# State-space mixer: the pooling branch by token, its moving means as products with a constant band matrix, and the projected blocks read back on GpSimd's queue

## Chip, cores, metric

One core of a Trainium2 chip runs the whole program. The metric is the device time of one execution in microseconds (us). Engines are named as in the profile: PE is TensorE's matmul stream, PEld its weight loads, DVE is VectorE, ACT is ScalarE, POOL is GpSimd, SP is SyncE, which here only issues DMAs.

## What is computed

The program is a trunk of two layers over 512 tokens of width 1024. Each layer has a SwiGLU network, a mixer and a second SwiGLU network. The change lies in the mixer of layer 0:

```python
z = hn @ ab_w_in[i]                                   # (512, 1024)
ya = pool_mixer(z[..., :512], pool_w[i], pool_scale[i])
yb = s5_mixer(z[..., 512:], ...)                      # bidirectional complex-diagonal scan
m = concatenate([ya, yb], -1) @ ab_w_out[i]

def pool_mixer(u, w_grp, scale):                      # 4 groups of 128 channels
    for gi, w in enumerate((2, 4, 8, 16)):            # windows, centred, cut off at the ends
        start, end = clip(t - w//2, 0, L), clip(t - w//2 + w, 0, L)
        p[gi] = (cs[end] - cs[start]) / (end - start) - u[group gi]
    return einsum('blgc,gcd->blgd', p, w_grp) * scale
```

So the pooling branch takes, for each channel, the mean over a window of tokens minus the token itself, and then a 128x128 product per group.

## The kernel before

Every product of two float32 matrices is written as three products of split operands: hi.hi, lo.hi and hi.lo (`mm3`, L179). ACT makes each hi by a cast, and DVE the lo by subtracting hi from the source. Weights go through the same split in the class `Weights`: `hi` (L117) on ACT, `lo` (L128) on DVE, four or five tiles ahead of their use. Each engine works its own queue strictly in the order in which the Python code issues.

`mixer` (L1335) stands at 393 to 540 us of the span. First, `first_proj` (L362) projects the four state-space blocks; the columns of `xT` (the normed tokens, channels on partitions) are kept in the order "mix", by place in a chunk of 8 tokens and then by chunk. `chunk_rows` (L1365) copies each block out of PSUM on ACT and writes it to `z_dram`; `u_rows` (L1374) reads two blocks at a time back on SP's queue into `us`, eight tokens of a chunk on partitions.

Then four units `ct` of the scan run through five steps: `inject` (L1384, PE: 32 small products from `us` and the table `cm` into the only `ps_x` buffer), `decay` (L1396, ACT), `scan` (L1403, DVE, a generator that yields in three places), `permute` (L1431, ACT) and `output` (L1438, PE 48 small products, then GELU on ACT and a DMA out). In this text a scan has a part A (L1410 and L1411, which read `ps_x`), a part B (L1413, L1414 and four scans L1419) and a part C (L1421, L1422 and four L1427, which write `s`). `inject` of the next unit must wait for part A, since `ps_x` has one buffer.

Between them stands the pooling branch. `pool_tile(i)` (L1468) projects a group on PE (24 products of 512 columns, channels on partitions), copies it twice on ACT with a reordering to plain token order (L1479, L1480), and sums the window by doubling on POOL (L1485, L1489, L1494, L1496); `rest` splits the result on ACT and DVE (L1500, L1501). `pool_out(i)` (L1505) multiplies by the group's 128x128 weights and splits again (L399, L400). `out_a` (L1513) accumulates the output projection. The hand-written order of all this is L1521 to L1581.

Of the kernel before, what the change touches and what calls it, by code (L numbers as in the profile page):

```python
# [7 lines left out]
F32 = mybir.dt.float32  # L8
# [7 lines left out]
P = 128  # L16
# [157 lines left out]
class Builder:  # L174
# [126 lines left out]
    def to_xT(self, xn, pair, gain, order, between, by_tile=False):  # L301
# [12 lines left out]
        for b in range(KT // 2):  # L314
            if not by_tile:
                ps[b] = self.bank("ps_t")
            for kt in (2 * b, 2 * b + 1):
                for i in range(by_tile, 2):
                    transpose(kt, i)
            if b % 2 == 1:  # L320
                for kt in (2 * b - 2, 2 * b, 2 * b - 1, 2 * b + 1):
                    src = ps[kt // 2][:, kt % 2 * 256:(kt % 2 + 1) * 256]
                    if order == "mix":
                        src = src.rearrange("p (c j) -> p j c", j=8)
                    elif order == "att":
                        src = src.rearrange("p (r c) -> p c r", r=4)
                    hi, lo = (self.part(x[:, kt, :], order, pair) for x in self.xT)
                    g = self.gcol[:, gain * KT + kt:gain * KT + kt + 1]
                    nc.scalar.activation(out=hi, in_=src, func=AF.Copy, scale=g)
                    V.scalar_tensor_tensor(out=lo, in0=src, scalar=g, in1=hi.bitcast(F32),  # L330
                                           op0=ALU.mult, op1=ALU.subtract)
            if b == 1 and between:
                between()


    def part(self, x, order, pair):

# [997 lines left out]
    def mixer(self, nxt, before):  # L1335
# [3 lines left out]
        xh, xl = self.xT  # L1339
        edge, scol, bcol = self.mix_small  # L1340
        con = {}
# [14 lines left out]
        def start():  # L1356
            nonlocal yp, y, yhl, sp, us
            yp = tc.alloc_tile_pool(name="mix_y", bufs=1)
            y = yp.tile([P, 4, SEQ], F32, name="y")
            yhl = [yp.tile([P, 4, SEQ], F32R, name=n) for n in ("y_hi", "y_lo")]  # L1360
            sp = tc.alloc_tile_pool(name="mix", bufs=1)
            us = sp.tile([P, 32, 64], F32, name="us")
            load("m0", "e0")

        def chunk_rows(ct, ps):  # L1365

            zt = sp.tile([P, SEQ], F32, tag="yt", bufs=2, name="zt")
            nc.scalar.copy(zt, ps)
            rows = self.z_dram[ct * P:(ct + 1) * P]
            nc.scalar.dma_start(rows, zt)  # L1370
            if ct == 2:
                u_rows(0)

        def u_rows(ct):  # L1374
            nc.sync.dma_start(us[:, 8 * ct:8 * ct + 16], self.by_chunk(self.z_dram[ct * P:(ct + 2) * P]))

        yp = y = yhl = sp = us = None
        self.first_proj(4, "mix", before, start, chunk_rows)
        load("m1")
        u_rows(2)  # L1380
        load("m2", "e1", "i0")
# [85 lines left out]

        def pool_tile(i):  # L1468

            w = self.W.take()  # L1470
            ps = self.bank("ps_p")
            self.proj(ps, w, "mix")
            pad, win = 16, self.POOL_W[i]
            z, s = (sp.tile([P, SEQ + 2 * pad], F32, tag="pz%d" % k, bufs=1, name="pz") for k in range(2))
            p = sp.tile([P, SEQ], F32, tag="pp", bufs=2, name="pp")
            by_token = ps.rearrange("p (j c) -> p j c", j=8)
            G.memset(z[:, :pad], 0.0)
            G.memset(z[:, pad + SEQ:], 0.0)
            nc.scalar.copy(z[:, pad:pad + SEQ].rearrange("p (c j) -> p j c", j=8), by_token)  # L1479
            nc.scalar.activation(out=p.rearrange("p (c j) -> p j c", j=8), in_=by_token, func=AF.Copy,  # L1480
                                 scale=float(win))
            o, e = 0, SEQ + 2 * pad
            for step in range(i + 1):
                if step == 0:
                    G.tensor_tensor(out=s[:, 1:], in0=z[:, 1:], in1=z[:, :-1], op=ALU.add)  # L1485
                    o = 1
                else:
                    h = 1 << (step - 1)
                    G.tensor_tensor(out=s[:, o + h:e - h], in0=z[:, o:e - 2 * h], in1=z[:, o + 2 * h:e], op=ALU.add)  # L1489
                    o, e = o + h, e - h  # L1490
                z, s = s, z
            for k, (a, b) in enumerate(((0, win // 2), (SEQ - win // 2 + 1, SEQ))):
                if b > a:
                    G.tensor_tensor(out=z[:, pad + a:pad + b], in0=z[:, pad + a:pad + b],  # L1494
                                    in1=edge[:, i, 8 * k:8 * k + b - a], op=ALU.mult)
            G.tensor_tensor(out=p, in0=z[:, pad:pad + SEQ], in1=p, op=ALU.subtract)  # L1496

            def rest():
                hl = [v[:, i] for v in yhl]
                nc.scalar.copy(hl[0], p)  # L1500
                V.tensor_tensor(out=hl[1], in0=p, in1=hl[0].bitcast(F32), op=ALU.subtract)  # L1501

            return rest

        def pool_out(i):  # L1505
            ps = self.bank("ps_A" if i < 3 else "ps_p")
            self.mm3(ps, [z[:, i * P:(i + 1) * P] for z in w_pool], [v[:, i] for v in yhl], True, True)
            self.split_evac(xh[:, i], xl[:, i], ps, scol[:, i:i + 1])

# [11 lines left out]
        for i, win in enumerate(self.POOL_W):  # L1521
            G.tensor_scalar(out=scol[:, i:i + 1], in0=scol[:, i:i + 1], scalar1=1.0 / win, scalar2=None, op0=ALU.mult)
        rest = [pool_tile(0)]
        decay(0)
        decay(1)
        inject(0)
        load("g0")
        for _ in scan(0):
            pass
        rest.append(pool_tile(1))  # L1530
        rest[0]()
        decay(2)
        inject(1)
        load("m3", "e2")
        for _ in scan(1):
            pass
        rest.append(pool_tile(2))
        rest[1]()
        permute(0)
        decay(3)  # L1540
        inject(2)
        load("i1", "g1")
        self.W.done()
        output(0)
        turn = scan(2)
        next(turn)
        rest[2]()
        self.W.done()
        y_rows(0)
        load("e3", "g2")  # L1550
        for _ in turn:
            pass
        rest.append(pool_tile(3))
        permute(1)
# [10 lines left out]
        rest[3]()  # L1565
        self.W.done()
        permute(2)
        out_a(range(3), range(2))
        next(turn)
        pool_out(3)  # L1570
        for _ in turn:
            pass
        output(2)
        permute(3)
# [3 lines left out]
        y_rows(2)  # L1578
        self.W.done(2)
        output(3)  # L1580
# [61 lines left out]
    def mid_weights(self, ly):  # L1642
        w = self.ins
        if ly == 0:
            l = [w["w_in"][i] for i in (4, 5, 6, 7, 0, 1, 2, 3)] + [w["w_pool"]]
            l += [w["w_ao"][0, i] for i in range(2)] + [w["w_glu"][i] for i in range(2)]
            return l + [w["w_ao"][0, i] for i in (2, 3)] + [w["w_ao"][1, i] for i in range(4)]
# [6 lines left out]
    def build(self):  # L1654
        tc, nc = self.tc, self.nc
        with ExitStack() as ctx:
# [9 lines left out]
            self.mix_small = [self.base.tile([P, *n], F32, name="mix_" + k)  # L1666
                              for k, *n in (("edge", 4, 16), ("scol", 4), ("bcol", 4))]
            self.h = self.base.tile([P, TT, D], F32, name="h")
# [12 lines left out]
    def first_norm(self, gain, order):  # L1681
# [5 lines left out]
        step(1)  # L1687
        edge, scol, bcol = self.mix_small
        nc.gpsimd.dma_start(edge, self.ins["pool_edge"].partition_broadcast(P))
        nc.gpsimd.dma_start(scol, self.ins["pool_sc"])  # L1690
# [61 lines left out]
def lay_out(inputs):  # L1752
# [25 lines left out]

    edge = np.zeros((4, 16), np.float32)
    for i, w in enumerate(Builder.POOL_W):  # L1780
        edge[i, :w // 2] = [w / (t + w // 2) for t in range(w // 2)]
        edge[i, 8:7 + w // 2] = [w / (w - 1 - k) for k in range(w // 2 - 1)]
    lanes = lambda z: z.reshape(2, 16, 2, 64, -1).transpose(2, 3, 0, 1, 4).reshape(P, 32, -1)
# [13 lines left out]
        "glu_b": a["ssm_b_glu"][0].reshape(4, P).T,  # L1797
        "pool_edge": edge,
        "w_in": col_tiles(a["ab_w_in"][0]),
        "w_pool": np.concatenate([a["pool_w"][0].transpose(1, 0, 2).reshape(P, HALF),  # L1800
# [31 lines left out]
```

## Time and profile before

| | us |
|---|---|
| median of 3 runs | 1886.88 (1886.74 to 1887.07) |
| the profiled execution's own time | 1886.41 |
| its span | 1884.6 |
| PE busy | 1831.5 (97%) |
| DVE busy | 1470.7 (78%) |
| ACT busy | 925.7 (49%) |
| POOL busy | 350.4 (19%) |

The span runs from the first to the last instruction; the execution's own time has 1.8 us more around it. Busy shares are means over the whole program: a stage of 70 us can be bound by another engine than the program is.

### The profile page before, as it was taken

Reading aid. Unit: us, or ns where it says so; the run is one execution under the profiler, and the core shown is the slowest. Engines: PE = TensorE matmul, PEld = TensorE weight load, DVE = VectorE, ACT = ScalarE, POOL = GpSimd, SP = SyncE. Lnnn points to the kernel's source line nnn. Section 1 sums busy time; section 2 is a strip of 40 time slices with the busy share of each in tenths; the row PEclk is TensorE's granted clock in tenths of the full one; section 3 lists DMA queues with packets and bytes.
Section 4 is the critical chain, followed back from the end, with each engine's and each line's share of the span. In section 5 each row is a group of like instructions: output and inputs, shape, how many; then the busy total and the mean of one; then the engine's idle time right before and its main releaser. Section 6 shows DMA issues by size and latency. Waiting matters only on the chain.

```text
span 1884.6 us, 31563 instructions
## 1 busy us (share of the span) xinstructions
PE 1831.5 (97%) x12368; PEld 1639.3 (87%) x12368; DVE 1470.7 (78%) x2380; ACT 925.7 (49%) x1749; POOL 350.4 (19%) x238
## 2 busy tenths in 40 slices
PE   7999999998899999999999999999999999999998
PEld 7887987787689999988999998888878789999886
DVE  6888989868779999844899996465565589999744
ACT  5254446354455444543644445355555465444532
POOL 2021322015011233200122320012222012322100
PEclk9999999999999999999999999999999999999999
DMA  6474346647432333332233324323222132333321
GB/s 196 128 224 165 110 137 194 202 132 256 161 125 79 101 112 102 107 107 78 94 109 102 103 89 135 101 80 122 90 93 99 62 106 96 102 106 102 123 96 62
DMA packets 82021, 225.48 MB, mean 120 GB/s; under 512 B 15792, under 2 KB 20048, under 8 KB 80848
## 3 DMA queue, kind: packets, MB, share of 16 engines
q1 hardware_dynamic: 70176, 197.80, 31.8%
q0 software_dynamic: 6960, 23.57, 4.1%
q10 hardware_dynamic: 4736, 2.10, 0.4%
q8 instruction: 97, 1.59, 0.4%
q14 instruction: 52, 0.43, 0.1%
HBM read 206.69 MB, written 18.84 MB: 120 GB/s over the span
## 4 chain that ended last, share of the span: by engine, by line
PE 62%; DVE 7%; ACT 3%; issue 1%; DMA 1%; DVEq 0%; ACTq 0%
PE ps_gu L183 10%; PE ps_gu L182 10%; PE ps_gu L181 10%; PE ps_A L183 3%; PE ps_A L182 3%; PE ps_A L181 3%; PE ps_B L182 3%; PE ps_B L181 3%; PE ps_B L183 3%; PE ps_f L181 3%; PE ps_f L182 2%; PE ps_f L183 2%; DVE w_lo L135 1%; PE ps_qk L899 1%; ACT junk L237 1%
## 5 line engine op out<-in xcount | busy, mean ns | idle before, releaser
L135 DVE TENSOR_TENSOR w_lo<-w_raw,w_hi 128x1024 fp32r<-128x1024 f32 x214 | 283.3, 1329 | 215.8 <-ACT w_hi L124 215.6
L124 ACT CAST w_hi<-w_raw 128x1024 fp32r<-128x1024 f32 (+1 forms) x313 | 262.9, 864 | 286.4 <-PE ps_A L183 71.3
L183 PE MATMUL ps_gu<-xT_hi,w_lo 128*128 128x256 f32 (+1 forms) x1008 | 307.5, 305 | 2.5 <-DVE w_lo L135 2.5
L183 PE MATMUL ps_gu<-xsum,w_lo 128*128 128x256 f32 x1088 | 308.2, 283 | 0.6 <-DVE w_lo L135 0.6
L182 PE MATMUL ps_gu<-xsum,w_hi 128*128 128x256 f32 x1088 | 307.8, 283 | 0.2 <-DVE xsum L518 0.2
L181 PE MATMUL ps_gu<-xsum,w_hi 128*128 128x256 f32 x1088 | 307.6, 283 | 0.0
L181 PE MATMUL ps_gu<-xT_hi,w_hi 128*128 128x256 f32 (+1 forms) x1008 | 304.9, 302 | 0.0
L182 PE MATMUL ps_gu<-xT_lo,w_hi 128*128 128x256 f32 (+1 forms) x1008 | 304.5, 302 | 0.0
L183 PEld LDWEIGHTS ps_gu<-xsum,w_lo 128*128 128x128 f32 x1088 | 208.6, 192 | 0.9 <-DVE w_lo L135 0.8
L182 PEld LDWEIGHTS ps_gu<-xsum,w_hi 128*128 128x128 f32 x1088 | 208.5, 192 | 0.4 <-DVE xsum L518 0.4
L181 PEld LDWEIGHTS ps_gu<-xsum,w_hi 128*128 128x128 f32 x1088 | 208.4, 192 | 0.0
L183 PEld LDWEIGHTS ps_gu<-xT_hi,w_lo 128*128 128x128 f32 x1008 | 190.4, 189 | 15.0 <-DVE w_lo L135 4.1
L181 PEld LDWEIGHTS ps_gu<-xT_hi,w_hi 128*128 128x128 f32 x1008 | 190.2, 189 | 8.5 <-issue 0.9
L182 PEld LDWEIGHTS ps_gu<-xT_lo,w_hi 128*128 128x128 f32 x1008 | 190.2, 189 | 7.3
L135 POOL TENSOR_TENSOR w_lo<-w_raw,w_hi 128x1024 fp32r<-128x1024 f32 x31 | 74.1, 2390 | 562.2 <-ACT w_hi L124 532.1
L109 POOL TENSOR_TENSOR w_u<-w_raw,w_s 128x512 f32<-128x512 f32 x64 | 112.2, 1754 | 354.9 <-ACT w_hi L124 196.3
L124 ACT CAST w_hi<-w_s 128x512 fp32r<-128x512 f32 x136 | 77.8, 622 | 197.3 <-DVE w_s L105 193.5
L105 DVE TENSOR_TENSOR w_s<-w_raw,w_u 128x1024 f32<-128x1024 f32 x68 | 145.8, 2144 | 2.3
L640 POOL TENSOR_TENSOR g<-g,m 128x1024 f32<-128x1024 f32 x34 | 94.6, 2782 | 244.9 <-DVE m L638 244.9
L181 PE MATMUL ps_B<-w_hi,gT 128*128 128x512 f32 x352 | 137.1, 389 | 1.6 <-DVE free L1264 1.6
L183 PE MATMUL ps_A<-w_hi,gT 128*128 128x512 f32 x352 | 137.1, 389 | 1.1 <-DVE gT L693 1.1
L181 PE MATMUL ps_A<-w_hi,gT 128*128 128x512 f32 x352 | 137.3, 390 | 0.0
(376 smaller groups left out, 4251.2 us busy)
## 6 DMA issues: line engine op xcount, KB each, us to landing
w_raw<-in_w_gu_dram SPq DMA_DIRECT2D x106, 512.0 KB, 3.4
w_raw<-in_w_dn_dram SPq DMA_DIRECT2D x88, 512.0 KB, 3.3
w_u<-in_w_gu_dram SPq DMA_DIRECT2D x70, 512.0 KB, 3.7
w_raw<-in_w_qk_dram SPq DMA_DIRECT2D x16, 512.0 KB, 3.3
bias<-in_att_bias_dram SPq DMA_DIRECT2D x16, 512.0 KB, 4.1
w_raw<-in_w_in_dram SPq DMA_DIRECT2D x8, 512.0 KB, 3.3
cm<-m_dram SPq DMA_DIRECT2D x4, 1024.0 KB, 8.7
w_raw<-in_w_ao_dram SPq DMA_DIRECT2D x8, 512.0 KB, 3.9
```

What stands on the lines that cost most here:

```text
L105: tt(out=blocks(s), in0=g[:, :HALF].unsqueeze(1).broadcast_to([P, 2, HALF]), in1=blocks(u)[:, :2], op=ALU.subtract)
L109: (h_engine or self.nc.gpsimd).tensor_tensor(out=z["h"], in0=g[:, HALF:], in1=z["s"][:, HALF:], op=ALU.add)
L124: self.nc.scalar.copy(hi[:, k:k + step], src[:, k:k + step])
L135: (engine or self.lo_engine).tensor_tensor(out=lo[:, :n], in0=src, in1=hi[:, :n].bitcast(F32), op=ALU.subtract)
L181: mm(ps, a[0], b[0], start=start, stop=False)
L182: mm(ps, a[0], b[1], start=False, stop=False)
L183: mm(ps, a[1], b[0], start=False, stop=stop)
L237: self.nc.scalar.activation(out=junk[:, :src.shape[-1]], in_=src, func=AF.Square, scale=scale, accum_out=out)
L640: nc.gpsimd.tensor_tensor(out=rows(f), in0=rows(f), in1=m, op=ALU.mult)
L899: nc.tensor.matmul(ps[:, :n], tq[rows], lo[rows], start=False, stop=True)
```

## The change

The pooling half of `z` is projected with tokens on partitions: `pool_rows` takes `xT` as the stationary operand and the weights (`w_pin`, laid out by rows) as the moving one, 24 products for each of four blocks of 128 tokens, as many as before. `split_evac` splits each block into hi and lo out of PSUM (ACT and DVE). `pool_means(i)` then forms the moving means as products of those blocks with a constant band matrix that comes from DRAM: for each token block two products (hi, lo) of 120 or 128 columns, six of 8 columns for the two ends of the sequence, and two of 8 columns for each neighbour block. That makes 20 products for the first group and 26 for each other one, 98 in all. The POOL work of `pool_tile` and its two ACT copies are gone.

Columns of `xT` are now in plain token order; the reordering moves into the copy of `chunk_rows`. Each projected block is read back by itself on POOL's queue instead of two at a time on SP's. `band` is loaded on POOL's queue in `start` and cast on ACT ahead of the first `chunk_rows`. On SP's queue the load of the second `cm` stands earlier. The lo parts of the pooling branch are collected in `lows` and issued at chosen places of the scans.

```diff
         def start():
...
-            load("m0", "e0")
+            raw = sp.tile([P, 640], F32, name="band")
+            G.dma_start(raw, ins["pool_band"])
+            band = [sp.tile([P, n], F32R, name="band" + k) for k, n in (("_hi", 640), ("_lo", 64))]
+            nc.scalar.copy(band[0], raw)
+            V.tensor_tensor(out=band[1], in0=raw[:, 576:], in1=band[0][:, 576:].bitcast(F32), op=ALU.subtract)
+            load("m0", "e0", "m1")
 
         def chunk_rows(ct, ps):
             zt = sp.tile([P, SEQ], F32, tag="yt", bufs=2, name="zt")
-            nc.scalar.copy(zt, ps)
+            nc.scalar.copy(zt.rearrange("p (j c) -> p j c", j=8), ps.rearrange("p (c j) -> p j c", j=8))
             rows = self.z_dram[ct * P:(ct + 1) * P]
             nc.scalar.dma_start(rows, zt)
-            if ct == 2:
-                u_rows(0)
+            G.dma_start(us[:, 8 * ct:8 * ct + 8], self.by_chunk(rows))
...
+        def pool_rows(ts, kts):
+            for kt in kts:
+                if kt // 2 == len(wz):
+                    wz.append(self.W.take())
+                for t in ts:
+                    if kt == 0:
+                        psz[t] = self.bank("ps_A" if t < 3 else "ps_p")
+                    self.mm3(psz[t], [x[:, kt, t * P:(t + 1) * P] for x in (xh, xl)], [x[:, kt % 2 * HALF:(kt % 2 + 1) * HALF] for x in wz[kt // 2]],
+                             kt == 0, kt == KT - 1)
+
+        def pool_means(i, later):
...
+            for k, (o, n, x, m) in enumerate(l):
+                nc.tensor.matmul(ps[:, o:o + n], x, m, start=k == 0, stop=k == len(l) - 1)
+            self.split_evac(*means[i], ps, None, later)
...
         decay(0)
+        pool_rows((0, 1), range(3))
+        inject(0)
+        pool_rows((0, 1), range(3, KT))
+        for t in range(2):
+            self.split_evac(*zs[t], psz[t], None, lows)
         decay(1)
-        inject(0)
         load("g0")
         for _ in scan(0):
             pass
-        rest.append(pool_tile(1))
-        rest[0]()
-        decay(2)
+        run_lows()
         inject(1)
         load("m3", "e2")
-        for _ in scan(1):
+        pool_rows((2, 3), range(KT))
+        self.W.done(4, fill=False)
+        turn = scan(1)
+        next(turn)
+        permute(0)
+        decay(2)
+        output(0)
+        for t in range(2, TT):
+            self.split_evac(*zs[t], psz[t], None, lows)
+        next(turn)
+        run_lows()
+        y_rows(0)
+        inject(2)
+        for _ in turn:
             pass
...
+        load("i1", "g1")
+        for i in range(4):
+            pool_means(i, lows)
+        self.W.fill(1)
+        load("e3", "g2")
         decay(3)
...
         turn = scan(2)
         next(turn)
...
+        run_lows()
         permute(1)
         inject(3)
         output(1)
...
-        for i in range(3):
-            pool_out(i)
+        for i in range(4):
+            pool_out(i, lows)
+        next(turn)
+        run_lows()
+        for _ in turn:
+            pass
+        self.W.fill(3)
+        self.W.done(fill=False)
         turn = scan(3)
```

On DVE, the second scan (unit 1) and what follows it up to the third. `t` holds the scan's work, `s` its result; `y_lo`, `xT_lo` are lo parts of the pooling branch, `w_lo` that of a weight tile. Before:

```order
L1410 TENSOR_TENSOR t_4430<-ps_x,ce 128x1024
L1411 TENSOR_TENSOR t_4431<-ps_x,ce 128x1024
L1413 TENSOR_TENSOR t_4430<-t_4430,t_4431 128x512
L1414 TENSOR_TENSOR t_4430<-t_4430,t_4431 128x512
L1419 SCALAR_TENSOR_TENSOR t_4430<-rho,t_4430 128x256 x4
L1421 TENSOR_TENSOR t_4431<-t_4430,ce 128x1024
L1422 TENSOR_TENSOR t_4430<-t_4430,ce 128x1024
L1427 TENSOR_TENSOR s<-t_4430,t_4431 64x8x64 x4
L1501 TENSOR_TENSOR y_lo<-pp,y_hi 128x512
L135 TENSOR_TENSOR w_lo<-w_raw,w_hi 128x1024
L1410 TENSOR_TENSOR t_4591<-ps_x,ce 128x1024
```

And with the change:

```order
L1414 SCALAR_TENSOR_TENSOR t_4461<-rho,t_4461 128x256 x4
L393 TENSOR_TENSOR xT_lo<-ps_A,xT_hi 128x512
L393 TENSOR_TENSOR xT_lo<-ps_p,xT_hi 128x512
L1416 TENSOR_TENSOR t_4462<-t_4461,ce 128x1024
L1417 TENSOR_TENSOR t_4461<-t_4461,ce 128x1024
L1422 TENSOR_TENSOR s<-t_4461,t_4462 64x8x64 x4
L135 TENSOR_TENSOR w_lo<-w_raw,w_hi 128x1024
L1405 TENSOR_TENSOR t_4702<-ps_x,ce 128x1024
L1406 TENSOR_TENSOR t_4703<-ps_x,ce 128x1024
L393 TENSOR_TENSOR y_lo<-ps_A,y_hi 128x512 x2
L393 TENSOR_TENSOR xT_lo<-ps_A,xT_hi 128x512
L393 TENSOR_TENSOR xT_lo<-ps_p,xT_hi 128x512
```

Line numbers here are those of the changed kernel: L1405 and L1406 are part A, L1408 to L1414 part B, L1416 to L1422 part C, L393 the lo of `split_evac`. Two lo parts, which read PSUM (token blocks 2 and 3), now stand inside scan 1 between its parts B and C, and those of the means stand inside scan 2 behind its part A.

On ACT, what stands around the first GELU (`yt`) and the first weight cast behind it, in the change:

```order
L1451 ACTIVATE yt<-ps_y 128x512
L1452 DMA y_dram<-yt 128x8x64
L392 CAST xT_hi<-ps_A 128x512
L392 CAST xT_hi<-ps_p 128x512
L392 CAST y_hi<-ps_A 128x512 x2
L392 CAST xT_hi<-ps_A 128x512
L392 CAST xT_hi<-ps_p 128x512
L124 CAST w_hi<-w_raw 128x1024
```

The casts of blocks 2 and 3 stand behind the GELU, and the cast of the weight tile, whose `w_lo` DVE does ahead of scan 2, stands behind the casts of all four means.

## Rows read from the trace of the kernel before

**Rows 1.** Windows of 10 us: PE, PEld, DVE, ACT, POOL busy, PE's clock, DMA; sum of 430:500.
```profile
470.00:480.00 10.00, 4.20 (x37) 3.19 (x33) 9.75 (x13) 5.47 (x8) 0.86 (x1) 0.77 0.74 250
...
sum 70.00, PE 57.04 PEld 48.02 DVE 65.36 ACT 34.83 POOL 23.60; mean PE 8.15 PEld 6.86 DVE 9.34 ACT 4.98 POOL 3.37
```
**Rows 2.** The chain that ended last, 478 to 497 us: start, duration, what.
```profile
482.34 0.60 DVE y_lo L1501
482.94 1.14 DVE w_lo L135
...
487.63 0.64 DVE xT_lo L400
...
493.63 0.45 PE ps_y L1453 x8
```
**Rows 3.** Timeline of DVE: start, duration, what, how many.
```profile
431.69 1.23 DVE L1410 TENSOR_TENSOR t<-ps_x,ce 128x1024 f32<-128x1024 f32 x1 [3.79 <-PE ps_x L1392]
...
434.08 0.69 DVE L1413 TENSOR_TENSOR t<-t,t 128x512 f32<-128x512 f32 x1
...
437.76 1.23 DVE L1421 TENSOR_TENSOR t<-t,ce 128x1024 f32<-128x1024 f32 x1
...
441.20 4.58 DVE L1427 TENSOR_TENSOR s<-t,t 64x512 f32<-64x512 f32 x4
...
488.19 1.21 DVE L1421 TENSOR_TENSOR t<-t,ce 128x1024 f32<-128x1024 f32 x1
...
490.77 2.81 DVE L1427 TENSOR_TENSOR s<-t,t 64x512 f32<-64x512 f32 x4
493.60 1.29 DVE L1466 TENSOR_TENSOR y_lo<-y,y_hi 128x512 fp32r<-128x512 f32 x2
```
**Rows 4.** Timeline of PE, mixer: start, duration, what; idle before in brackets.
```profile
424.10 0.40 PE L182 MATMUL ps_p<-xT_lo,w_hi 128*128 128x512 f32 x1
424.33 0.40 PE L183 MATMUL ps_p<-xT_hi,w_lo 128*128 128x512 f32 x1
...
429.56 2.08 PE L1392 MATMUL ps_x<-us,cm 128*64 128x64 f32 x64
...
478.82 0.80 PE L181 MATMUL ps_A<-w_hi,xT_hi 128*128 128x512 f32 x1 [5.80 <-DVE xT_lo L400]
...
485.45 0.34 PE L1449 MATMUL ps_y<-us,perm 128*64 128x64 f32 x4
...
488.40 0.50 PE L181 MATMUL ps_A<-w_hi,xT_hi 128*128 128x512 f32 x1
...
496.11 0.50 PE L181 MATMUL ps_x<-y_hi,w_hi 128*128 128x512 f32 x1
```
**Rows 5.** Timeline of ACT: a reordering copy, a weight cast, a GELU.
```profile
429.67 1.10 ACT L1479 COPY pz<-ps_p 128x512 f32<-128x512 f32 x1 [3.02 <-PE ps_p L183]
...
455.85 1.03 ACT L124 CAST w_hi<-w_raw 128x1024 fp32r<-128x1024 f32 x1
...
458.19 0.60 ACT L1456 ACTIVATE yt<-ps_y 128x512 f32<-128x512 f32 x1
```
**Rows 6.** Timeline of PE: narrow products; 128*64 means 64 stationary columns.
```profile
409.54 1.96 PE L308 MATMUL ps_t<-ident,xn 128*128 128x128 f32 x16 [0.79 <-ACT xn L297]
411.26 0.36 PE L181 MATMUL ps_p<-xT_hi,w_hi 128*128 128x256 f32 x1
...
1328.69 0.22 PE L181 MATMUL ps_o<-pt_hi,v_hi 128*64 128x128 f32 x1
1328.75 0.22 PE L182 MATMUL ps_o<-pt_lo,v_hi 128*64 128x128 f32 x1
```
**Rows 7.** DMA issues: what, queue, count, KB each, median us to landing.
```profile
z_dram<-zt ACTq DMA_DIRECT2D x4, 256.0 KB, 4.4
...
ssm_tab<-in_ssm_c_dram POOLq DMA_DIRECT2D x1, 512.0 KB, 3.7
...
free<-kept_lp POOLq DMA_DIRECT2D x1, 288.0 KB, 8.7
```

More of the change, by code (lines that the diff above doesn't have):

```diff
@@ L1466, in split_y @@
             V.tensor_tensor(out=lo, in0=y[:, ct], in1=hi.bitcast(F32), op=ALU.subtract)
[L1468 to L1503, printed above, removed]
@@ L1505, in pool_out @@
-        def pool_out(i):
-            ps = self.bank("ps_A" if i < 3 else "ps_p")
-            self.mm3(ps, [z[:, i * P:(i + 1) * P] for z in w_pool], [v[:, i] for v in yhl], True, True)
-            self.split_evac(xh[:, i], xl[:, i], ps, scol[:, i:i + 1])
+        zs = [[x[:, t] for x in yhl] if t < 2 else [x[:, 2 + t] for x in (xh, xl)] for t in range(TT)]
+        means = [[x[:, 2 + i] for x in yhl] if i < 2 else [x[:, 4 + i] for x in (xh, xl)] for i in range(4)]
+        psz, wz = {}, []
+        def pool_rows(ts, kts):
[7 more added lines that the diff above has]
+                             kt == 0, kt == KT - 1)
@@ L1510, in mixer, with pool_out @@
+        def pool_out(i, later):
+            ps = self.bank("ps_A" if i < 3 else "ps_p")
+            self.mm3(ps, [z[:, i * P:(i + 1) * P] for z in w_pool], means[i], True, True)
+            self.split_evac(xh[:, i], xl[:, i], ps, scol[:, i:i + 1], later)
         lhs = lambda kt: (xh[:, kt], xl[:, kt])
@@ L1560, in mixer @@
         w_pool = self.W.take()
-        for i in range(3):
-            pool_out(i)
+        for i in range(4):
[6 more added lines that the diff above has]
+        self.W.done(fill=False)
         turn = scan(3)
         next(turn)
-        rest[3]()
-        self.W.done()
         permute(2)
         out_a(range(3), range(2))
-        next(turn)
-        pool_out(3)
+        output(2)
         for _ in turn:
             pass
-        output(2)
         permute(3)
@@ L1578, in mixer @@
         y_rows(2)
-        self.W.done(2)
+        self.W.fill(4)
         output(3)
@@ L1777, in lay_out, with sums @@
     bias = bias.reshape(16, 4, P, 256).transpose(0, 2, 1, 3)
-    edge = np.zeros((4, 16), np.float32)
+    token = np.arange(P)[:, None]
+    band, ends = np.zeros((P, 4, 144), np.float32), np.zeros((P, 4, 2, 8), np.float32)
     for i, w in enumerate(Builder.POOL_W):
-        edge[i, :w // 2] = [w / (t + w // 2) for t in range(w // 2)]
-        edge[i, 8:7 + w // 2] = [w / (w - 1 - k) for k in range(w // 2 - 1)]
+        def sums(t, o):
+            near = (t >= o - w // 2) & (t < o + w // 2)
+            n = np.minimum(o + w // 2, SEQ) - np.maximum(o - w // 2, 0)
+            return near * (np.float32(w) / n.astype(np.float32)) - np.float32(w) * (t == o)
+        band[:, i] = sums(P + token, P + np.arange(-8, 136)[None])
+        ends[:, i, 0] = sums(token, np.arange(8)[None])
+        ends[:, i, 1] = sums(SEQ - P + token, np.arange(SEQ - 8, SEQ)[None])
     lanes = lambda z: z.reshape(2, 16, 2, 64, -1).transpose(2, 3, 0, 1, 4).reshape(P, 32, -1)
```

66 lines of the change are left out of this document (32 added, 34 removed).

## Prediction, written before the changed kernel had run

> **What bounds the kernel now.** I read the windows of the mixer first. From 430 to 500 us DVE is busy for 65.4 of 70 us and PE for 57.0, and in the slice from 470 to 480 PE is busy for 4.2 of 10 us at a granted clock of 0.77, while DVE has 9.75 [rows 1]. So this stage hangs on DVE, though over the whole program PE is the busiest. The chain of waits says the same: in its last part before the output projection it stands on DVE, and it reaches PE only at 493.6 with the last `output` [rows 2]. The timeline of DVE then gives the prices. The first scan starts at 431.69, the last one ends at 493.60: 61.9 us [rows 3]. One scan left alone takes 2.39 us (part A, 431.69 to 434.08), 3.68 (part B, to 437.76) and 5.41 (part C, 488.19 to 493.60), together 11.5 [rows 3]. Four make 45.9. Four lo parts from the pooling tiles at 0.60, three weight lo parts at 1.14 and four lo parts behind `pool_out` at 0.64 [rows 2] add 8.4. That is 54.3 us of 61.9. The missing 7.6 us are instructions that ran longer beside POOL: the four L1427 took 4.58 us in scan 0, 2.81 us in scan 3, where POOL had nothing to do [rows 3]; POOL was busy for 23.6 us of the stage [rows 1].
>
> **What is removed.** POOL's sums go, and with them these 7.6 us of DVE. The two ACT copies of each pooling tile go too; ACT is busy for 35 of 70 us here [rows 1], so this is worth nothing by itself.
>
> **What is added on DVE.** Four lo parts become eight (four token blocks, four means). At 0.60 that is +2.4 us. DVE's own work becomes 54.3 + 2.4 = 56.7 us, 5.2 less than before.
>
> **What is added on PE.** The projection keeps 96 products of 512 columns at 0.233 us (424.10 to 424.33) [rows 4]. New are the 98 narrow products of the means, each with 128 stationary columns. No row of before shows such a product, so I bound it. With 64 stationary and 128 moving columns the pitch is 0.060 us (1328.69 to 1328.75); 16 transposes with 128 stationary columns took 1.72 us, from 409.54 until the next product began at 411.26, 0.107 each [rows 6]. Between 5.9 and 10.5 us in all. I take 0.107, since the stationary columns are as many, and since the weight load cannot hide behind 8 moving columns.
>
> **Where PE and DVE meet.** The new order makes DVE wait for PE through ACT in places where it waited for nothing. I lay the prices along the queues.
>
> *Start.* The band is loaded on POOL's queue once the transposes, the last readers of the memory under it, have ended: 409.54 + 1.96 = 411.5 [rows 6]. Loads on that queue took 3.7 to 8.7 us [rows 7]; I take 5, which with the issue gives 417. Its cast (estimate 0.7, by the weight cast of 1.03 for 1024 columns [rows 5]) stands ahead of the first block's copy on ACT. That copy now reorders: 1.10 us [rows 5]. Then 4.4 us to `z_dram` [rows 7] and again 5 for the readback: `us` is there at 429.0. PE has done 18 of its products by 428.3 and injects from 429.0 to 431.2 (2.08 [rows 4] and a gap). Before, scan 0 began at 431.7, now at 431.3: -0.4. With the two loads at 3.7 each PE's 428.3 decides (-0.7 more); at 8.7 each it is 435.7, +6.7. In `z_dram`'s wait only the other readbacks queue on POOL, so nothing else there is late.
>
> *First wait.* PE: 30 products (7.0), inject 1 (2.2), 48 products for blocks 2 and 3 (11.2), `output` 0 (2.9, as 485.45 to 488.40 [rows 4]): 454.5. ACT: GELU 0.60 [rows 5] and the issue of a DMA, then the casts of blocks 2 and 3, about 0.6 each: the first is done at 456.2. DVE: scan 0 to 442.8, two lo parts to 444.0, A and B of scan 1 to 450.1. There the lo parts of blocks 2 and 3 stand, and part C queues behind them. DVE idles 6.1 us, does the lo parts until 457.4 and part C until 462.8.
>
> *Second wait.* PE injects unit 2 until 456.7 and makes the means until 456.7 + 10.5 = 467.2. ACT casts the last one by 467.9 and only then the weight tile, by 468.9. The `w_lo` of that tile stands on DVE ahead of scan 2: idle from 462.8 to 468.9, 6.1 us; it is done at 470.0.
>
> *The rest.* Part A of scan 2 to 472.4, four lo parts to 474.8, part B to 478.5. PE can inject unit 3 only after part A, 474.6; `output` 1 to 477.5, twelve products of `pool_out` to 480.3. The last lo part ends at 481.7 instead of 481.1: wait of 0.6. Part C to 487.1, two `w_lo` to 489.4, scan 3 to 500.9.
>
> **The sum.** DVE: -5.2 + 6.1 + 6.1 + 0.6 - 0.4 = +7.2, 500.9 against 493.6. PE ends a little later: `out_a` waits for a `w_lo` until 488.2, and after such an idle time its clock is low: at 478.82, after 5.80 us of idling, 21 products took 6.63 us instead of 4.9 [rows 4]. So 4.2 + 1.7, `output` 2 with 2.9, 18 products with 4.2 and `output` 3 with 2.9 lead to 504.1. Before, the next work began at 496.11 [rows 4]. Behind it PE works without a gap, and the order is unchanged, so +8.0 us goes into the time. The profiled execution took 1886.41; with the change 1894.4, and the median of the runs stands 0.5 above it: **1894.9**.
>
> Loading the second `cm` earlier is worth nothing: `ps_x` and not `cm` held the injections. On SP's queue the last two weight tiles of the pooling half now stand behind that megabyte; PE needs them from 431 and 434 on, some 10 us behind their issue, which is the cover; without it their delay would come on top of the start. The copies of `xT` without reordering are the same work.
>
> **Rivals.**
>
> *The narrow products are cheap.* At 0.060 the means end at 462.6, the weight cast at 464.3: the second wait falls to 1.5 us, the third goes. Scan 3 ends at 495.7, `output` 3 at 498.9: +2.8, **1889.7**, inside what counts as no change. For it speaks that the 0.060 is a product of this program; against it, that its stationary operand has half the columns. The Trainium skill, "TensorE: Matmul & The Clock Gate", section "Back-to-back issue gap", gives a gap of about 56 ns at 128 and about 25 ns at 64 or fewer moving columns, which would make 3.4 us of the means, no second wait and an estimate of 1888; the same page, section "LDWEIGHTS (loading the stationary operand)", gives columns / 1.2, 107 ns here, and the 0.107 of the transposes agrees with the second. Chance 0.17.
>
> *DVE's own work decides, and the kernel is faster.* If PE were far enough ahead, DVE would simply lose its 7.6 us: -5.2 - 0.4, **1881.3**. It decides at one point, whether the casts of blocks 2 and 3 are done before DVE reaches 450.1. For that PE would have to be through with `output` 0 some 6 us earlier, in 24.3 us from 424.1 on where the rows give 30.4. Chance 0.07.
>
> *The readback on POOL's queue is the late one.* If band and readback take more than I chose, in a stretch with much other traffic, everything behind moves: up to +6.7 on the forecast, in the middle **1898.5**. For it: the band's cast stands ahead of the copy on ACT. Chance 0.14.
>
> *POOL is not what slows DVE.* Then the 7.6 us stay; those of scans 0 and 1 fall into the two waits, those of scan 2 (some 3) do not: **1898**. Against it: the long instructions stand only where POOL is busy. Chance 0.05.
>
> **Numbers.** A measurement of this kernel can tell about 0.2%, 3.8 us, from no change: 1883.1 to 1890.7. The forecast has 0.57. Slower: 0.57 less a little for a pitch between the bounds, and both late cases, 0.72; the same: the cheap products and that little, 0.20; faster 0.08. The range reaches from 1885.5, below the cheap products, to 1901, near the late end; outside lie the faster case and the last of the late ones, under 2 in 10.
>
> **What would show it.** Right: in the changed profile DVE has two idle times of about 6 us, one ended by the ACT cast of `xT_hi` (L392) and one by `w_hi` (L124); the four L1422 of each scan take near 2.8 us; the 98 products of L1500 stand about 0.107 apart; scan 3 ends near 501. Wrong: a pitch of 0.06 or less, no DVE idle time between scans, or the first scan starting later than 433. The whole would be wrong if PE were still the one that waits between 445 and 478.

## The result, and the profile after

| | before | with the change |
|---|---|---|
| median, us | 1886.81 (4 runs, 1886.65 to 1887.07) | 1908.12 (4 runs, 1906.57 to 1909.46) |
| ratio, 95% interval | | 1.0113 (1.0095 to 1.013) |
| profiled execution, its span | 1886.41, 1884.6 | 1907.08, 1905.3 |

Slower, as forecast, but by 21 us and not by 8: 13 us above the forecast and above its range. The windows of the change show where it went (columns as in [rows 1]):

```profile
460.00:470.00 10.00, 10.00 (x59) 10.00 (x58) 3.77 (x5) 1.76 (x3) 0.00 (x0) 0.62 0.56 182
470.00:480.00 10.00, 4.81 (x31) 4.75 (x31) 4.08 (x5) 4.49 (x8) 0.00 (x0) 0.50 0.18 59
540.00:550.00 10.00, 6.53 (x24) 4.94 (x23) 5.95 (x8) 4.99 (x9) 0.00 (x0) 0.88 0.56 163
```

DVE, which had 9.75 of 10 us in the slice from 470 to 480 [rows 1], has 4 us in both slices. PE is busy without a gap from 460 to 470, but its granted clock is 0.62 on average. The third line is a place that the prediction did not look at at all. DVE's timeline, to be read beside [rows 3]:

```profile
432.12 1.23 DVE L1405 TENSOR_TENSOR t<-ps_x,ce 128x1024 f32<-128x1024 f32 x1 [0.46 <-PE ps_x L1387]
...
440.70 2.80 DVE L1422 TENSOR_TENSOR s<-t,t 64x512 f32<-64x512 f32 x4
...
457.34 0.69 DVE L393 TENSOR_TENSOR xT_lo<-ps_A,xT_hi 128x512 fp32r<-128x512 f32 x1 [6.58 <-ACT xT_hi L392]
...
475.92 1.23 DVE L135 TENSOR_TENSOR w_lo<-w_raw,w_hi 128x1024 fp32r<-128x1024 f32 x1 [12.07 <-ACT w_hi L124]
...
487.81 2.07 DVE L396 SCALAR_TENSOR_TENSOR xT_lo<-ps_A,mix_scol,xT_hi 128x512 fp32r<-128x512 f32 x3 [2.46 <-ACT xT_hi L395]
...
506.71 2.80 DVE L1422 TENSOR_TENSOR s<-t,t 64x512 f32<-64x512 f32 x4
```

The L1422 of scan 0 take 2.80 us instead of 4.58: POOL's interference is gone, as forecast. The three waits are those of the forecast, in their places and with their releasers: 6.58 (forecast 6.1), 12.07 (6.1) and 2.46 us (0.6). The second one's size comes from PE's timeline, to be read beside [rows 4] and [rows 6]:

```profile
406.43 1.97 PE L308 MATMUL ps_t<-ident,xn 128*128 128x128 f32 x16 [0.93 <-ACT xn L297]
...
457.42 0.32 PE L1500 MATMUL ps_A<-band_hi,y_hi 128*128 128x120 f32 x1
...
457.70 0.23 PE L1500 MATMUL ps_A<-band_hi,y_hi 128*128 128x8 f32 x1
457.78 0.25 PE L1500 MATMUL ps_A<-band_lo,y_hi 128*128 128x8 f32 x1
457.89 0.25 PE L1500 MATMUL ps_A<-band_hi,y_lo 128*128 128x8 f32 x1
458.00 0.31 PE L1500 MATMUL ps_A<-band_hi,y_hi 128*128 128x128 f32 x1
...
473.75 0.35 PE L1500 MATMUL ps_p<-band_hi,xT_hi 128*128 128x8 f32 x1
473.97 0.35 PE L1500 MATMUL ps_p<-band_hi,xT_lo 128*128 128x8 f32 x1
...
479.51 3.57 PE L1387 MATMUL ps_x<-us,cm 128*64 128x64 f32 x64 [5.19 <-issue]
...
546.59 0.50 PE L181 MATMUL ps_B<-w_hi,xT_hi 128*128 128x512 f32 x1 [3.47 <-ACT junk L237]
```

The pitch of the narrow products is 0.11 us at first (457.89 to 458.00) and 0.22 at the end (473.75 to 473.97). Finer windows of the same stretch give the clock:

```profile
457.00:462.00 5.00, 5.00 (x58) 4.86 (x53) 4.58 (x6) 1.38 (x3) 0.00 (x0) 1.00 0.68 175
463.00:474.00 11.00, 11.00 (x54) 11.00 (x53) 0.83 (x2) 1.17 (x2) 0.00 (x0) 0.50 0.23 88
```

From 457 to 462 it is 1.00 (2.4 GHz), from 463 on 0.50 (1.2 GHz), and in both stretches PE was busy with narrow products all the time. The 98 products took some 16.8 us (457.4 to 474.2) instead of 10.5. Last, the start, from ACT's and POOL's timelines:

```profile
409.06 0.56 POOL L1360 DMA_DIRECT2D band<-in_pool_band_dram  x1 [10.73 <-ACT xT_hi L327]
415.97 0.73 ACT L1362 CAST band_hi<-band 128x640 fp32r<-128x640 f32 x1 [5.10 <-DMA band<-in_pool_band_dram]
416.61 0.58 ACT L1369 COPY zt<-ps_p 128x512 f32<-128x512 f32 x1
```

ACT stood 5.10 us in front of the band's cast, and the first block's copy behind it. From the transposes to that copy it is 10.2 us (406.43 to 416.61).

### The profile page after: what moved, and what is told of

Its sections match the earlier page's. It is cut to its first block, busy times and chain, and to the rows that moved or that the text cites. A ratio compares the mean times of both kernels' runs of the same rounds, so it can differ in the third digit from the quotient of the medians.

```text
span 1905.3 us, 31740 instructions
## 1 busy us (share of the span) xinstructions
PE 1847.8 (97%) x12466; PEld 1654.7 (87%) x12466; DVE 1466.0 (77%) x2385; ACT 921.1 (48%) x1746; POOL 330.2 (17%) x213
## 4 chain that ended last, share of the span: by engine, by line
PE 60%; DVE 8%; ACT 3%; issue 2%; DMA 1%; DVEq 0%; ACTq 0%
PE ps_gu L183 10%; PE ps_gu L181 10%; PE ps_gu L182 10%; PE ps_A L182 3%; PE ps_A L183 3%; PE ps_A L181 3%; PE ps_B L183 3%; PE ps_B L182 3%; PE ps_B L181 3%; PE ps_f L181 3%; PE ps_f L182 2%; PE ps_f L183 2%; DVE w_lo L135 2%; ACT junk L237 1%; PE ps_qk L895 1%
## 5 line engine op out<-in xcount | busy, mean ns | idle before, releaser
L182 PE MATMUL ps_A<-w_lo,gT 128*128 128x512 f32 x352 | 137.0, 389 | 0.0
```

The costliest lines, as they stand in the source:

```text
L182: mm(ps, a[0], b[1], start=False, stop=False)
```

## Experiments

Theory: (1) the clock fell under products of 8 columns, and that doubled the second wait; (2) the wait at 546.59 comes of the order in which PSUM tiles are first used; (3) the band's cast delays the start; (4) the waits swallow one another and do not add up. The rivals stand in the expectations, which were written before each run.

In all traces I read four marks: T, the start of the second pair's transposes (406.43 above, 409.54 in [rows 6]); S, the first L1405 of scan 0 behind T (before: 431.69 in [rows 3]); W, from there to the end of the last L1422 of scan 3 (506.71 + 2.80 = 509.51 above); and G, from the fourth GELU to the first transposes of the next norm. T differs from run to run (402.3 to 409.6 in the change and the twelve runs), so that T + S, W and G, each read from one trace of a run, tell more of an edit than a median does. Ratios are to the kernel before on the same chip.

| run | ratio (95%) | S | W | G |
|---|---|---|---|---|
| before | 1 | 22.2 | 61.9 | 51.8 |
| the change | 1.0113 (1.0095 to 1.013) | 25.7 | 77.4 | 57.0 |
| e1_edge_late | 0.9991 (0.9982 to 1.0001) | 22.2 | 61.9 | 52.0 |
| e2_banks | 1.0093 (1.0076 to 1.011) | 28.2 | 79.0 | 52.0 |
| e3_wide | 1.0129 (1.0105 to 1.0152) | 27.2 | 81.7 | 53.6 |
| e4_wpool | 1.0089 (1.0066 to 1.0112) | 26.2 | 71.0 | 57.1 |
| e5_bandlate | 1.0092 (1.0077 to 1.0108) | 20.5 | 79.0 | 57.1 |
| e6_merge | 1.0076 (1.0061 to 1.0091) | 27.2 | 67.8 | 58.2 |
| e7_lows | 1.0122 (1.0103 to 1.0141) | 25.2 | 77.4 | 56.7 |
| e8_all | 0.9958 (0.9942 to 0.9974) | 20.6 | 58.7 | 51.8 |
| e9_w128 | 1.0099 (1.0084 to 1.0114) | 24.9 | 72.3 | 56.7 |
| e10_98 | 1.0024 (1.0013 to 1.0035) | 20.5 | 67.6 | 51.8 |
| e11_spq | 0.9989 (0.998 to 0.9999) | 26.1 | 58.5 | 51.8 |
| e12_pool_lo | 0.9961 (0.9949 to 0.9974) | 20.5 | 60.4 | 52.6 |

**What the narrow products do to the clock.** First, wide products put between them:

```diff
             for k, (o, n, x, m) in enumerate(l):
                 nc.tensor.matmul(ps[:, o:o + n], x, m, start=k == 0, stop=k == len(l) - 1)
+                if k % 4 == 3:
+                    nc.tensor.matmul(junk, xh[:, 0, :P], xh[:, 1], start=True, stop=True)
...
+        junk = self.bank("ps_y")
         for i in range(4):
```

> The changed kernel, with 24 more products on PE: behind every fourth narrow product of the means one of 512 columns, whose result nobody reads (the output is unchanged). Theory: PE's granted clock fell to 0.50 from 463 us on because PE did nothing but narrow products. With wide ones between them it stays at 1.00, a narrow product keeps its 0.111 us, and the means take 98 x 0.111 + 24 x 0.233 = 16.5 us, no more than the 16.9 without the extra work; time within 1 us of 1908, or 1 to 3 us less because inject 3 and pool_out run at full clock. Rival: the clock falls for another reason (what ran before, the load on the chip): narrow products still at 0.213 us, wide ones at 0.47, means 26 us or more, time 1917.

Neither came out whole. The windows of this run:

```profile
463.00:475.00 12.00, 12.00 (x92) 11.25 (x90) 6.25 (x8) 1.50 (x3) 0.00 (x0) 1.00 0.54 172
477.00:482.00 5.00, 5.00 (x21) 4.61 (x20) 0.00 (x0) 0.00 (x0) 0.00 (x0) 0.50 0.00 0
```

The clock held until 476, 13 us after the first narrow product instead of 5, and then fell all the same. The means took 19 us (with 23 wide products, not the 24 of the expectation). Wide neighbours put the fall off in this trace; they did not prevent it. DMA traffic is not needed for the fall: from 472 to 482 the DMA share is 0.00, while in the next run the clock held beside shares of 0.9 (461 to 465). Next, the same number of products, none of them with 8 columns:

```diff
-                a, b = 8 * (t == 0), P - 8 * (t == TT - 1)
+                a, b = 0, P
                 l += [(P * t + a, b - a, x, rhs(a, b - a)) for x in rows(t)]
...
+            l = [(o, n, x, m) if n > 8 else (P * (k % 4), P, x, rhs(0, P)) for k, (o, n, x, m) in enumerate(l)]
             for k, (o, n, x, m) in enumerate(l):
```

> The changed kernel, in which every one of the 98 products of the means moves 120 columns or more: the 66 of 8 columns are replaced by products of 128 columns with the same stationary operand (so the contributions at the sequence's ends and of the neighbour blocks are left out of the means and others are added in their place; the output is not the reference's). As many weight loads, 3.3 times the moved columns. Theory A: the clock fell because most of the 98 products moved only 8 columns; now it stays at 1.00, the means take 98 x 0.111 = 10.9 us instead of 16.9, the wait in front of the w_lo ahead of scan 2 falls from 12.1 to about 6 us, and the time to 1902, although PE does more. Theory B: any product bound by its weight load lets the clock fall; it falls to 0.50 some 3 to 5 us after the first one, the means take 17 us, the time is 1908.

Theory A held in this trace. The window over the means, and DVE's second wait:

```profile
459.00:470.00 11.00, 11.00 (x98) 10.89 (x97) 6.10 (x8) 1.93 (x4) 0.00 (x0) 1.00 0.58 184
```

```profile
471.70 1.23 DVE L135 TENSOR_TENSOR w_lo<-w_raw,w_hi 128x1024 fp32r<-128x1024 f32 x1 [6.49 <-ACT w_hi L124]
```

98 products in 11 us at clock 1.00, and a wait of 6.49 us where the prediction had 6.1. PE moved 2.8 times the columns (98 x 128 against 66 x 8 and 32 of 120 or 128; the 3.3 of the expectation was miscounted) in two thirds of the time. W fell by 5.1 us, and the time, 1903.58, was 1.6 above what was expected. It is one trace, and the interval of the ratio overlaps that of the change. Six traces have the 98 products as in the change (the change, e2, e4, e5, e7 and e10): in each the clock fell, 3 to 6 us behind the first of them. So, as far as seven traces show it, the fall goes with the products of 8 columns; why is open.

Then the fewest products:

```diff
+            zero = sp.tile([P, SEQ], F32R, name="zero")
+            nc.scalar.mul(zero, raw[:, :SEQ], 0.0)
...
-            l = []
+            l = [(0, SEQ, rows(0)[0], zero)]
             for t in range(TT):
-                a, b = 8 * (t == 0), P - 8 * (t == TT - 1)
+                a = 8 * (t == 0) - 8 * (t > 0 and half > 1)
+                b = P + 8 * (t < TT - 1) - 8 * (t == TT - 1)
...
-            for t in range(TT):
-                if t > 0 and half > 1:
-                    l += [(P * t - 8, 8, x, rhs(-8, 8)) for x in rows(t)]
-                if t < TT - 1:
-                    l += [(P * t + P, 8, x, rhs(P, 8)) for x in rows(t)]
```

> The changed kernel, with the products of a token block and of its two neighbours merged (one product of 128 to 144 columns instead of three of 8, 120 or 128 and 8): 56 products instead of 98, and one of 512 columns with zeros in front of each group, which opens the accumulation. The sums are the same. Theory: each narrow product costs its weight load, 0.111 us at full clock and 0.213 at half, however few columns it moves; 4 x 0.233 + 56 x 0.111 = 7.2 us if the clock stays up, about 11 if it falls after 5 us as before, instead of 16.9. The wait in front of the w_lo ahead of scan 2 (12.1 us) falls by 6 to 10 us, the time to 1898 to 1902. Rival: the products of 8 columns cost little and the time goes into the moved columns: 98 products move 5888 columns in all with the change and 7424 with this, so no gain, 1908.

The theory held: the means from 459.3 to 466.6, the clock at 1.00 in the window, and DVE's wait ahead of scan 2 down from 12.07 to 2.52 us. W fell by 9.6 us, the time is 1899.10. The time fell by less than W: S is 27.2 here, and the zeros are made on ACT ahead of the first copy (0.6 us). The expectation's counts of columns are wrong (4,496 and 6,544, zeros included, are right); its rival has no place for a gain either way.

```profile
459.00:466.00 7.00, 7.00 (x68) 6.76 (x65) 6.39 (x8) 2.39 (x5) 0.00 (x0) 1.00 0.78 220
```

```profile
468.20 1.22 DVE L135 TENSOR_TENSOR w_lo<-w_raw,w_hi 128x1024 fp32r<-128x1024 f32 x1 [2.52 <-ACT w_hi L124]
```

**Which waits count.** The first wait taken away:

```diff
         next(turn)
-        run_lows()
         y_rows(0)
         inject(2)
         for _ in turn:
             pass
+        run_lows()
```

> The changed kernel, with the two lo parts of token blocks 2 and 3 moved from inside scan 1 to behind it. Prediction's first term read as an addition: the wait of 6.6 us in front of them goes and the time falls by 6. Theory: the waits are not added up, the later one swallows the earlier: DVE ends scan 1 some 5 us earlier, then waits as much longer in front of the w_lo ahead of scan 2, because the end of the means on PE is what it waits for. The first wait is under 1 us, the second 17, scan 2 begins at the same distance from scan 0 as before (45 us), time within 1 us of 1908. If the later lo parts hold up the means on PE (these read them), it is 1 us slower.

```profile
455.70 0.69 DVE L393 TENSOR_TENSOR xT_lo<-ps_A,xT_hi 128x512 fp32r<-128x512 f32 x1 [1.24 <-ACT xT_hi L392]
...
474.39 1.23 DVE L135 TENSOR_TENSOR w_lo<-w_raw,w_hi 128x1024 fp32r<-128x1024 f32 x1 [17.40 <-ACT w_hi L124]
```

The theory held to the tenth: 5.3 us less in the first place, 5.3 more in the second, W unchanged at 77.4. What sets W up to there is PE's chain to the end of the means, not DVE. Then the second wait:

```diff
+        self.W.fill(1)
         for i in range(4):
             pool_means(i, lows)
-        self.W.fill(1)
```

> The changed kernel, with the cast and the lo part of the weight tile w_pool asked for ahead of the four means instead of behind them. Prediction's sum read literally (a wait of 12.1 us in front of w_lo goes): -12, 1896. Theory: the end of the means (474.3 us) is what DVE waits for; the w_lo (1.2 us) and part A of scan 2 (2.4 us) move into that wait, and DVE then waits for the casts of the means in front of their lo parts: -3.6, 1904.5. Rival: nothing is won, because PE's inject 3 needs part A and comes behind the means anyway: 1908.

```profile
463.99 0.69 DVE L393 TENSOR_TENSOR xT_lo<-ps_A,xT_hi 128x512 fp32r<-128x512 f32 x1 [1.08 <-ACT xT_hi L392]
469.54 0.69 DVE L393 TENSOR_TENSOR xT_lo<-ps_p,xT_hi 128x512 fp32r<-128x512 f32 x1 [4.86 <-ACT xT_hi L392]
```

The wait moved to the lo parts of the means, as the theory had it. W fell by 6.4 us where 3.6 was expected, some 2 of them because scan 0 began later against PE's work in this execution: the first GELU stands 21.6 us behind it (450.02) and not 23.5, which also made the first wait 4.61 us. The median, 1903.4, is 1.1 below the expectation.

**The start.** The band's cast behind the copies:

```diff
         def start():
...
-            nc.scalar.copy(band[0], raw)
-            V.tensor_tensor(out=band[1], in0=raw[:, 576:], in1=band[0][:, 576:].bitcast(F32), op=ALU.subtract)
...
+        nc.scalar.copy(band[0], raw)
+        V.tensor_tensor(out=band[1], in0=raw[:, 576:], in1=band[0][:, 576:].bitcast(F32), op=ALU.subtract)
         for i, win in enumerate(self.POOL_W):
```

> The changed kernel, with the band's cast (ACT) and lo part (DVE) issued behind the four blocks' copies instead of ahead of the first. Measured from the second pair's transposes (T), because T itself stood anywhere from 402.3 to 409.6 us in the traces so far: scan 0 began at T + 22.2 in the kernel before and at T + 25.7, 26.2, 27.2 and 28.2 with the change. Theory: this delay is ACT's 5 us wait for the band, which holds up the first copy (T + 10.2 instead of T + 5.6), the readback and the weight casts behind it. Then scan 0 begins near T + 22, and since PE moves with it, the whole stage gets shorter by 3 to 5 us. Rival: the readback on POOL's queue or the late weight loads hold it as well: T + 25 or later, no gain.

S is 20.5, 5.2 less than with the change and 1.6 less than before; the ratio is 0.0021 lower, some 4 us. The first copy stands at T + 5.6 (409.71 with T at 404.09). So the band's cast held up the start. The early load of the second `cm` makes no difference to S, as predicted: it is 20.5 with that load here and 20.6 without it in the run with all mends (e8).

**PSUM, and the load that the change drops.**

```diff
         self.new_psum(ps_x=(1, 1024), ps_y=2, ps_p=1, ps_A=3)
+        for name in ("ps_p", "ps_x", "ps_y", "ps_y"):
+            self.bank(name)
```

> The changed kernel, with the PSUM tiles of the mixer asked for in the order that the kernel before used first (ps_p, ps_x, ps_y, then ps_A). Theory: the wait of 3.47 us in front of the first ps_B product (546.59 us) is there because the changed kernel uses ps_A first, so that the banks of ps_B are now those of ps_A, which are read last. Then the wait is gone, the clock of 0.88 and 0.95 behind it too, and the time falls by 5 us, to 1903. Rival: the wait comes of the later start of the work (loads that arrive late, casts behind it), not of the banks: 1908, wait still there.

The wait is gone, with no other edit: G falls from 57.0 to 52.0, the kernel before has 51.8, and the median is 1903.77 (the ratio 0.0020 lower, some 4 us). The first two ps_B products, without an idle time ahead of them:

```profile
548.55 0.40 PE L181 MATMUL ps_B<-w_hi,xT_hi 128*128 128x512 f32 x1
548.78 0.39 PE L182 MATMUL ps_B<-w_lo,xT_hi 128*128 128x512 f32 x1
```

Then the load of the edge factors, moved in the kernel before:

```diff
+        G.dma_start(edge, ins["pool_edge"].partition_broadcast(P))
...
-        nc.gpsimd.dma_start(edge, self.ins["pool_edge"].partition_broadcast(P))
```

> The kernel before, with its only small load of the window's edge factors (pool_edge, 32 KB in 128 broadcast pieces) issued at the beginning of the mixer instead of within the first 3 us of the program. Theory: this load, which the change drops, is why the changed kernel reached the mixer 3.1 us earlier (second pair's transposes at 406.4 instead of 409.5 us): its small packets hold up the first weights (first weight cast 10.80 us before, 9.40 after), PE idles longer and its clock is 0.83 from 10 to 20 us. Then this kernel takes 1883.7 us (-3.1), and its first weight cast stands near 9.4. Rival: the 3.1 us come from elsewhere (scatter of the start, or another removed work of POOL): 1886.8, cast at 10.8.

Not settled. The first weight cast stood at 8.40 us and T at 404.8, but the median is only 1.6 us lower, the interval reaches from -0.18% to +0.01%, and T reached 409.6 in another run without the load.

**All mends together**, with `load("m1")` back behind `first_proj` and the lo parts of the means behind part B of scan 2 as the only edits not shown yet:

> The changed kernel with all of the mends at once: PSUM tiles in the order before, w_pool's cast ahead of the means, lo parts of blocks 2 and 3 behind scan 1, those of the means behind part B of scan 2, merged products, band's cast behind the copies, and the second cm loaded where it was. Theory: with T the second pair's transposes, scan 0 begins at T + 21, DVE has no wait above 1 us until scan 2, scan 3 ends at T + 79 instead of T + 84.0 in the kernel before, and the time is 1882 to 1884: faster than before by 3 to 5 us, what the prediction's unhindered DVE (-5.2) gives. Rival: PE is the bound of this order, with the clock falling in the means and in the gaps: scan 3 ends at T + 88 or later, 1890.

```profile
426.00 1.23 DVE L1405 TENSOR_TENSOR t<-ps_x,ce 128x1024 f32<-128x1024 f32 x1 [2.14 <-PE ps_x L1387]
...
451.40 0.69 DVE L393 TENSOR_TENSOR xT_lo<-ps_A,xT_hi 128x512 fp32r<-128x512 f32 x1 [1.41 <-ACT xT_hi L392]
...
466.82 2.07 DVE L396 SCALAR_TENSOR_TENSOR xT_lo<-ps_A,mix_scol,xT_hi 128x512 fp32r<-128x512 f32 x3 [0.64 <-ACT xT_hi L395]
...
481.90 2.80 DVE L1422 TENSOR_TENSOR s<-t,t 64x512 f32<-64x512 f32 x4
```

1876.62 us, ratio 0.9958: faster than both kernels. Scan 3 ends at T + 79.3 (84.0 before), as expected, with waits of 1.4 and 0.6 us left. The stage as traced (S + W, and what follows up to the next norm) is 3.0 us shorter than before; the other 5 us of the median lie ahead of it and behind it in the traces, and what they are was not separated (T alone stood 4.1 us earlier in this trace than in that of before).

The merged means undone, the rest kept:

> The kernel with all mends, but with the 98 products of the means as in the change. Theory: with everything else mended the narrow products alone cost 16.9 instead of 7.4 us on PE, and DVE waits for them in front of the lo parts of the means: scan 3 ends 8 to 9 us later than with the merged ones (T + 88 instead of T + 79.3), time 1884 to 1886, no better than the kernel before. Rival: the order was what mattered, DVE has slack there: within 2 us of 1876.6.

1889.16 us, ratio 1.0024; scan 3 ends at T + 88.1. The clock again falls under the 98 products, and DVE waits for the last mean:

```profile
452.00:457.00 5.00, 5.00 (x46) 4.93 (x45) 4.82 (x6) 1.49 (x2) 0.00 (x0) 1.00 0.76 202
458.00:467.00 9.00, 9.00 (x44) 9.00 (x44) 3.98 (x7) 0.59 (x1) 0.00 (x0) 0.50 0.80 313
```

```profile
468.36 0.69 DVE L393 TENSOR_TENSOR xT_lo<-ps_p,xT_hi 128x512 fp32r<-128x512 f32 x1 [4.86 <-ACT xT_hi L392]
```

The median is 3 us above the expectation, W as expected. So the form of the means alone is worth 9 us of W, the whole gain over the kernel before and more. Now the queue of the readback undone, the rest kept:

```diff
-            G.dma_start(us[:, 8 * ct:8 * ct + 8], self.by_chunk(rows))
+            nc.sync.dma_start(us[:, 8 * ct:8 * ct + 8], self.by_chunk(rows))
```

> The kernel with all mends, but with the four blocks read back on SP's queue (one at a time) instead of POOL's. Theory: on SP's queue the readback of a block waits for its write to z_dram (5.3 us) and the loads of the pooling weights queue behind it, so that PE gets them later: scan 0 begins at T + 22 to T + 24 instead of T + 20.6, and the time rises by 1 to 4 us, to 1878 to 1880. Rival: the queue does not matter because PE's own work ahead of inject 0 decides (scan 0 at T + 20.6, time 1876.6).

S is 26.1 instead of 20.6, the time 6 us more: the theory's direction, more than its size. ACT waited 4.13 us for a pooling weight, as against 1.34, PE 2.8 us for the copy behind it. So for blocks read back one at a time POOL's queue was the better one, which the band's cast hid in the change; two blocks at a time on SP's queue, as in the kernel before (S 22.2), were not tried in this order. The last one:

```diff
-        self.W.fill(1)
+        self.W.fill(1, G)
...
         w_pool = self.W.take()
+        self.W.fill(3, G)
...
-        self.W.fill(3)
```

> The kernel with all mends, with the lo parts of the three weight tiles of this stage (w_pool, two of the output projection) on POOL, which has no other work there, and the last two asked for ahead of pool_out. Theory: DVE loses 3 x 1.2 = 3.6 us, PE's waits of 1.9 and 2.2 us ahead of the output projection go, POOL at 2.4 us for each slows DVE's own instructions beside it by 1 to 2 us in all: scan 3 ends at T + 76.5 to T + 78 instead of T + 79.3, time 1874 to 1876. Rival: POOL's work slows DVE by as much as it takes off it: T + 79 or later, 1877 or more.

No gain (1876.74), but in the traced execution not for the rival's reason: in it the clock fell under the merged means too, and the third wait was long:

```profile
455.00:458.00 3.00, 3.00 (x17) 2.96 (x17) 3.00 (x6) 0.59 (x1) 0.00 (x0) 0.57 0.93 373
458.00:462.00 4.00, 4.00 (x71) 3.98 (x72) 3.69 (x5) 3.52 (x7) 0.00 (x0) 0.50 1.00 363
```

```profile
468.74 2.07 DVE L396 SCALAR_TENSOR_TENSOR xT_lo<-ps_A,mix_scol,xT_hi 128x512 fp32r<-128x512 f32 x3 [5.20 <-ACT xT_hi L395]
```

Inject 3 ran at 0.50 and took 3.68 us instead of 2.08, and two weight casts of 1.0 us each now stood ahead of `pool_out`'s casts on ACT. What POOL's help is worth stays open. Of the four runs with merged means the clock held in three.

## Why the prediction was right in direction and wrong in size

- **POOL's 7.6 us: right.** Every scan runs at the prices of scan 3. In e12, where POOL works again, two L1422 beside it took 1.78 us (471.48), and in e8, without it, 1.39. The Trainium skill, "SBUF — State Buffer", section "SBUF: two separate sides", says that DVE, in an instruction with two SBUF inputs, and GpSimd share a pair of ports that one of them holds for a whole instruction; the 4.58 us beside POOL and the 2.80 without it agree, for an instruction with two such inputs (`s<-t,t`).
- **The waits: places and releasers right.** The sum laid along the queues put the second wait behind the first one's absolute end. e7 shows that this was the way to do it: the 6.1 + 6.1 were never two independent prices, and up to scan 2 PE's work sets the time, not DVE's.
- **The step that failed: "makes the means until 456.7 + 10.5 = 467.2".** The pitch was right at full clock (0.11; e9: 98 in 11 us, wait 6.49). But the prediction applied a low clock only behind an idle time (478.82, [rows 4]) and held 0.107 for a PE without gaps. 16.8 us instead of 10.5 make the second wait 12.07: +6.0 us. Its bounds, 5.9 and 10.5, had no end for a low clock.
- **The third wait, 2.46 for 0.6: +1.9.** PE idled 5.19 us in front of inject 3 and then took 3.39 us for it (479.51 to 482.90) instead of 2.08, at a clock of 0.51. The low clock after an idle time was priced for `out_a` and not here. In the change the clock was low already, from the means on; in e6 and e9 it was 1.00 to their end, fell to 0.50 in the same idle time, and the third wait was 2.49 and 2.41 us.
- **The start: too short by 3.9, hidden by luck.** S was 25.7, where the prediction has 431.3 - 409.5 = 21.8: the band's cast came at T + 9.5 and not at T + 7.5, the readback took 6.5 us to land and not 5 (median of the four issues), and inject 0, behind 4.02 us of idling, 3.40 us instead of 2.08. The reordering copy cost 0.58 and not 1.10: [rows 5] shows a copy that writes with a stride, this one reads with one. T came 3.1 us earlier than in the trace of before, by scatter or because a load was dropped (e1), so scan 0 was only 0.8 late. The bound for late loads was miscounted as well: two loads at 8.7 us instead of 5 make +7.4 and not +6.7.
- **What was not in the sum at all: PSUM, +5.2.** G grew from 51.8 to 57.0. I read the order of instructions and not the order in which the PSUM tags are first used. e2 changed that order alone, and the wait was gone; that the banks of `ps_B` otherwise lie on those of `ps_A` is the explanation, which no trace shows. "Behind it PE works without a gap, and the order is unchanged" was the sentence that failed.

The account: scan 3 ended at 509.5 and not at 500.9, 8.6 us, of which the three waits and the start make 6.0 + 1.9 + 0.5 + 0.8 = 9.2 (DVE's own work was 0.6 shorter). With 5.2 for PSUM that is 13.8; the median missed by 13.2.

Of the rivals, "the readback is the late one" had the right place (S) and the wrong culprit: the queue helps (e11), the cast ahead of the copy hurts (e5). "The narrow products are cheap" fell. Of the two sections of the Trainium skill cited there, the gap of about 25 ns for few columns ("Back-to-back issue gap") is not what the 8-column products show (0.08 and 0.11 us, 457.70 to 458.00): the section gives it for single products, without the time of a weight load. Columns / 1.2 for the weight load, 107 ns, agrees with the pitch of 0.11 us at full clock; at half clock it is 0.22.

## What to carry to other kernels

A form that turns one engine's work into many small products is to be costed at both clocks and not only by pitch and count: merging them was worth 9 us here where everything else was mended, and in the one trace of it as many products with 128 columns were done sooner than with mostly 8. Waits along a chain swallow one another; ask what the last one waits for before taking away the first. Check what a change does to the layout of pools (who uses a bank first) and what it puts ahead of a copy that others wait for: each of these cost some 5 us here (G in e2, S in e5), beside the 6 us of the slow means.

## What the runs showed that I had not expected

- PE's granted clock fell from 1.00 to 0.50 while PE was busy without a gap: after 5 us of mostly 8-column products in the change, after 13 us with wide ones between them, and not at all in 11 us of 128-column products (one trace). The Trainium skill, "TensorE: Matmul & The Clock Gate", section "HAM oscillation — how this bites in real kernels", names PE's idle gaps as what lets the clock fall. Here there was none, and the measurement decides. Why it fell in one of four runs with merged means (e12) was not settled.
- A narrow product with the stationary operand of the one ahead of it stands 0.08 us behind it (457.70 to 457.78), with another one 0.11 (457.78 to 457.89).
- A copy whose source in PSUM is strided and whose target is not took 0.58 us, no more than a plain one (0.59 in the kernel before).
- The distance from the start of the program to the mixer varied by 7 us between executions of kernels that do the same work there.
